# Turning activations into the next product's layout: ten of fourteen batches from TensorE transposes to VectorE block transposes and ScalarE moves

## The chip, the cores and the metric

The kernel runs on one core of one Trainium2 chip. Five engines work side by side, each from its own queue of instructions and in its order: TensorE (PE in the profile; its weight loads are PEld), VectorE (DVE), ScalarE (ACT), GpSimd (POOL), and SyncE (SP), which here does nothing but issue DMAs. The metric is the time of one execution on the device, in microseconds; the figure of a kernel is the median of several runs.

## The reference

One decoder layer over 256 tokens of 2048 channels, in float32. Three sub-layers follow each other, each on a normalised and modulated input, with a vector `mod` computed from a conditioning vector by a 2048 x 18432 product:

```python
mod = (silu(c) @ w_ada + b_ada).reshape(B, 9, 1, D)
h = modulate(rms_norm(x, g_ffn1), mod[:, 0], mod[:, 1])
x = x + 0.5 * mod[:, 2] * swiglu(h, w_ffn1_gu, w_ffn1_down)      # d_ff = 5632
h = modulate(rms_norm(x, g_mix), mod[:, 3], mod[:, 4])
u_pool, q, k, v, ga, gb = split(h @ w_in)
y_pool = multiscale_pool(u_pool, pool_mix, pool_scale) @ w_pool_up
y_attn = swa_sink_attention(q, k, v, ...) @ w_attn_up
merged = sigmoid(ga) * y_pool + sigmoid(gb) * y_attn
x = x + mod[:, 5] * (merged @ w_o)
h = modulate(rms_norm(x, g_ffn2), mod[:, 6], mod[:, 7])
x = x + 0.5 * mod[:, 8] * swiglu(h, w_ffn2_gu, w_ffn2_down)
```

with `swiglu(h) = (silu(h @ w_gate) * (h @ w_up)) @ w_down`.

## The kernel before

**Sets and ktiles.** Every large product is cut into sets. A set computes up to 1024 output columns for both token tiles (2 x 128 tokens) and walks the inner dimension in steps of 128 rows, called ktiles: 16 of them for inner dimension 2048, 44 for 5632. `Set.load` (L166) fetches 1 MB of weights by one DMA into a tile with the tag `raw`, of which there are six (`RAW = 6`): two ktiles of a 1024-wide set, four of a 512-wide one. `Set.prep` (L172) splits each ktile's float32 weights into a high half `wh`, cast on ScalarE (L180), and a low half `wl`, the difference taken on VectorE (L184); there are three buffers of each. `Set.mm` (L187) then runs, for each token tile, high x high (L194), low x high (L196) and high x low (L198): twelve matmuls for a 1024-wide ktile, six for a 512-wide one. The activations are the stationary operand and so must lie with their channels on the partitions. `run` (L205) walks a set and calls a hook after the ktile that the hook is registered for.

**Side work.** The `mod` vectors that are not needed at once are summed on VectorE while sets run: `ada_item` (L115) loads 1 MB of `w_ada` into another of the six `raw` tiles and adds it up by two instructions of 1024 columns (L129). `ada_side` sets how many such items follow each group of ktiles: 0.82 in the first FFN, 0.56 in the mixer, 0.15 in the second FFN.

**Turning.** A product's result has tokens on the partitions. In an FFN, for each block of 1024 columns (the last has 512), a gate set is followed by an up set; `silu_to` (L386, ScalarE) and `times` (L391, VectorE) leave the activated block in a tile `sg`, of which there is one. Before the down product it must be turned so that channels lie on the partitions, in the tile `actT` (tag `big`). `store_T` (L378) makes a list of pieces of two 128-channel blocks each; a piece, `pair_T` (L221), issues four 128x128 transposes on TensorE against an identity matrix (L225) into a PSUM bank and one copy on ScalarE (L382) from there to `actT`. `hook` (L397) registers the whole list behind ktile 3 of the next set. In the mixer the same is done by `tr` (L739) with the copy at L742: once per half of the merged block, during the gate-a set of the second half and during the first set of `w_o`.

There are fourteen such batches: three at once behind the first part of the first FFN, three more in that FFN (1024, 1024 and 512 columns), two in the mixer, six in the second FFN (five of 1024 columns, one of 512). The batch of columns 4096 to 5119 falls into the 512-wide gate set; the 512-column batch falls into the first set of the down product, whose activations are split by `split_stat` (L292; casts at L297, differences at L298).

**Order.** Each engine's order of instructions is fixed when the program is built, by a scheduler that weighs the order of the source against what it takes to be ready; so work can stand earlier in an engine's queue than its place in the source. Which buffer of a tag a tile gets is fixed then too, and the waits between engines follow from reads and writes.

Of the kernel before, what the change touches and what calls it, by code (L numbers as in the profile page):

```python
# [15 lines left out]
P = 128  # L16
D = 2048
# [22 lines left out]
def trunk_layer(ctx, tc, x, c, w_ada, b_ada, g_ffn1, w_ffn1_gu, w_ffn1_down, g_mix, w_in,  # L40
# [16 lines left out]

    # Eight PSUM banks in two groups of four: one holds the running set's accumulators, the
    # other serves everything small until the next set takes it.
    cur, rr = [0], [0]  # L60
# [7 lines left out]

# [1 line left out]
    ident = const.tile([P, P], F32, name="ident")  # L70
# [12 lines left out]

# [1 line left out]
    # Each partition sums its 16 rows of w_ada; a matrix of ones then sums the partitions.  # L85
    ada_v = w_ada[0].rearrange("(k p) n -> p k n", p=P)
# [12 lines left out]
    def mod_col(j, b, c0):  # L99
        """Sums that lie alike on all partitions, to a column for each 128 channels."""  # L100
        k, n = c0 // P, b.shape[1] // P
        d = t_([P, n, P], "t2", T2)
        nc.vector.tensor_tensor(d, b.rearrange("p (a q) -> p a q", a=n),
                                ident.unsqueeze(1).to_broadcast([P, n, P]), ALU.mult)
        m = mcol[:, j, k:k + n]
        nc.vector.tensor_reduce(m, d, AX.X, ALU.add)
        i, o = j // 3, j % 3
        bc = bcol[:, (2 * i + o) * KD + k:(2 * i + o) * KD + k + n]
        if o == 0:
            nc.vector.tensor_tensor(m, m, bc, ALU.add)  # L110
        else:
            nc.vector.scalar_tensor_tensor(out=m, in0=m, scalar=1.0, in1=bc, op0=ALU.add, op1=ALU.add)
            nc.vector.tensor_tensor(m, m, gcol[:, i * KD + k:i * KD + k + n], ALU.mult)

    def ada_item(j, c0, i, a):  # L115
        """An eighth of the sum for SW columns of one of the nine vectors."""
        if i == 0:
            a.append(t_([P, SW], "acc", 2))
            if j % 3 == 2:
                nc.gpsimd.memset(a[0], 0.0)  # L120
                nc.sync.dma_start(a[0][0:1, :], b_ada[0:1, j * D + c0:j * D + c0 + SW])
        raw = t_([P, 2, SW], "raw", RAW)
        nc.sync.dma_start(raw, ada_v[:, 2 * i:2 * i + 2, j * D + c0:j * D + c0 + SW])
        for k in range(2):
            sc = cs[:, 2 * i + k:2 * i + k + 1]
            if i == k == 0 and j % 3 != 2:
                nc.vector.tensor_scalar_mul(a[0], raw[:, k, :], sc)
            else:
                nc.vector.scalar_tensor_tensor(out=a[0], in0=raw[:, k, :], scalar=sc, in1=a[0],  # L129
                                               op0=ALU.mult, op1=ALU.add)  # L130
        if i < 7:
            return
        for o in range(0, SW, CW):
            b = bank()
            acc_sum(b, a[0][:, o:o + CW])
            if j % 3 == 2:
                if j not in gates:
                    gates[j] = t_([P, D], "gate", 1)
                nc.scalar.activation(gates[j][:, c0 + o:c0 + o + CW], b, AF.Copy, scale=1.0 if j == 5 else 0.5)
            else:  # L140
                mod_col(j, b, c0 + o)
# [12 lines left out]

# [1 line left out]
    class Set:  # L156
# [70 lines left out]

# [1 line left out]
    # sums of squares over D / 2, a last column holding twice EPS: their sum is twice the variance  # L229
    ssq = const.tile([P, T, 5], F32, name="ssq")  # L230
# [8 lines left out]
    def rsqrt2(v2, s0, r0, a):  # L239
        """r0 * a = 1 / sqrt(v2 / 2), by a Newton step from the engine's root."""  # L240
        nc.scalar.activation(s0, v2, AF.Sqrt, scale=0.5)
        nc.vector.reciprocal(r0, s0)
        if v2.shape[1] == 1:
            nc.vector.scalar_tensor_tensor(out=a, in0=v2, scalar=r0, in1=r0, op0=ALU.mult, op1=ALU.mult)
        else:
            nc.vector.tensor_tensor(a, r0, r0, ALU.mult)
            nc.vector.tensor_tensor(a, a, v2, ALU.mult)
        nc.vector.tensor_scalar(a, a, -0.25, 1.5, ALU.mult, ALU.add)
# [41 lines left out]

# [1 line left out]
    def split_stat(src, kept=None):  # L292
        """Halves of src, two ktiles at a time; some stay for another set if there is room."""
        cache = {}
# [32 lines left out]

    # ---- the last products of a phase and the first of the next, one token tile after the other,
    # so that each tile's sums, norm and transposes run under the other's products ----
    def tail(s, c0, jgate, after):  # L330
        """The last TAIL ktiles of a set; yields after each token tile's products."""
        items = []
# [45 lines left out]
    def store_T(src, f0, n, actT):  # L378
        """Transposes of act columns, to be called once the next set runs."""
        def dst(f, b):  # L380
            k = f0 // P + f
            nc.scalar.copy(actT[:, k:k + 2, :].rearrange("p a b -> p (a b)"), b)  # L382

        return [lambda f=f: pair_T(lambda t, f: src[:, t, f * P:(f + 1) * P], f, dst) for f in range(0, n // P, 2)]

    def silu_to(sg, g):  # L386
# [10 lines left out]
    def hook(fs):  # L397
        return {3: lambda: [f() for f in fs]} if fs else None

    def ffn(w_gu, w_down, hh, hl, actT, f0, pend, sg, g, jgate, after):  # L400
        """From act column f0 on, g holding the gate products there; up to the last set's tail."""
        stat = lambda k: (hh[:, k, :], hl[:, k, :])
        while f0 < DFF:
            fw = min(SW, DFF - f0)
            if sg is None:
                if g is None:
                    g = run(Set(w_gu, KD, (f0, fw), stat), hook(pend))
                    pend = []
                sg = t_([P, T, fw], "sg", 1)
                silu_to(sg, g)  # L410
                g = None
            times(sg, run(Set(w_gu, KD, (DFF + f0, fw), stat), hook(pend)))
            pend = store_T(sg, f0, fw, actT)
            sg = None
            f0 += fw
# [10 lines left out]

    # ---- first norm: its scale and shift come in column blocks, and with each block the
    # first sets of products go on; their sums wait in SBUF ----
    x_sb = const.tile([P, T, D], F32, name="x_sb")

    def ada_block(c0, w, shared):
        """The pieces of the first shift and scale at w columns. The rows of w_ada are summed on
        each partition, or, if shared, every other one goes through the tensor engine."""
        acc, banks = [], []
# [26 lines left out]
    nc.sync.dma_start(x_sb, x[0].rearrange("(t p) d -> p t d", p=P))  # L461
    # norm gains, pool scale and the biases of shifts and scales: a column for each 128 channels
    KG, KB = 3 * KD + PW // P, 6 * KD
# [68 lines left out]

# [1 line left out]
    WI = w_in[0]  # L534
    QO, KO, UO, GA, GB = PW, PW + NH * HD, 0, PW + NH * HD + 2 * NKV * HD, PW + NH * HD + 2 * NKV * HD + D

    # relative bias as a Toeplitz table in DRAM: column a holds distance a - 127
    rel = const.tile([NB + 1, NH], F32, name="rel")
# [63 lines left out]
    def qk_norm():  # L602
# [14 lines left out]
        for a in range(0, 8, 2):  # L617
            def dst(f0, b):
                nc.scalar.activation(qT[:, f0:f0 + 2, :].rearrange("p a b -> p (a b)"), b, AF.Copy, scale=gq[:, 0:1])
            pair_T(lambda t, f: q_sb[:, t, f * P:(f + 1) * P], a, dst)  # L620
        # keys and values in falling order of position
        b = bank()
# [47 lines left out]
    def heads_out(h0):  # L670
        l, kv = lg, h0 // 8
        pT = t_([P, 3, HB, P], "sg", 1)
        for i in range(HB):
# [3 lines left out]
            nc.scalar.copy(pT[:, :, i, :], b.rearrange("p (g q) -> p g q", g=3))  # L677
        # even heads fill the lower half of the partitions, odd heads the upper
        b1 = bank((P, 2, P))
# [43 lines left out]
    for half_ in range(2):  # L723
# [14 lines left out]

        def tr(sgb=sgb, half_=half_):  # L739
            def dst(f, b):  # L740
                k = half_ * 8 + f
                nc.scalar.copy(mT[:, k:k + 2, :].rearrange("p a b -> p (a b)"), b)  # L742
            for f in range(0, 8, 2):
                pair_T(lambda t, f: sgb[:, t, f * P:(f + 1) * P], f, dst)
        hk = {3: tr}
    residual(run(Set(w_o[0], KD, (0, SW), split_stat(mT)), hk), 0, 5, sumsq)
# [4 lines left out]

# [1 line left out]
    ov = out[0].rearrange("(t p) d -> p t d", p=P)  # L753
# [18 lines left out]
def _shape_constants():  # L772
    import numpy as np

    # pooling as a product over positions: mean over the window, less the token itself
    pw = np.zeros((4, P, TOE), np.float32)
    for g, w in enumerate(POOL_WINDOWS):
# [6 lines left out]
        pw[g, :, S:] = full[P:, P:]  # L784
    # bucket of each distance, one-hot; row NB marks what the window leaves out
    n = np.arange(TOE) - (P - 1)
# [33 lines left out]
```

## Time and profile before

| what | value |
|---|---|
| median of three runs | 2044.59 us (2043.46 to 2045.07) |
| span of the profiled execution | 2041.3 us |
| TensorE matmuls busy | 2008.7 us, 9053 instructions |
| VectorE busy | 1472.2 us, 1698 instructions |
| ScalarE busy | 987.3 us, 1324 instructions |
| read from HBM | 520.00 MB, 256 GB/s over the span |

The profiled execution's own time stands nowhere but in its span, from the first to the last instruction; the median of the runs is 3.3 us longer than that span, which is what lies around it. In the rows below, a row of a timeline gives the start in us, the duration, the engine, the line of the kernel, the operation, the tiles written and read, the shape and the count, and in brackets the idle time of the engine before it with what ended it. A row of the grouped lines gives, behind the bar, the busy time in us, the mean duration of one in ns, and the idle time before the group with what ended most of it. A row of waits gives who waited for whom, the us in total, how many times, and the longest.

### The profile page before, as it was taken

How to read it: one execution, taken by the hardware profiler on the slowest of the kernel's cores; microseconds unless marked ns; L12 is line 12 of the kernel's file. 1: busy time of each engine (PE TensorE's matmuls, PEld its weight loads, DVE VectorE, ACT ScalarE, POOL GpSimd, SP SyncE). 2: the span in 40 equal slices, each digit the busy share in tenths (PEclk: the TensorE clock that was granted, in tenths of full speed). 3: DMA queues.
4: the chain of work that ended last, by engine and by line, in shares of the span. 5: the costliest groups of instructions: out<-in, count | busy, mean ns of one | idle time of the engine just before them, and what ended most of it. 6: DMA issues, size and time to landing. Idle time of an engine off the chain costs nothing. (4 is left out here: it accounts for less than half of the span.)

```text
span 2041.3 us, 23823 instructions
## 1 busy us (share of the span) xinstructions
PE 2008.7 (98%) x9053; PEld 1648.5 (81%) x9053; DVE 1472.2 (72%) x1698; ACT 987.3 (48%) x1324; POOL 7.3 (0%) x17
## 2 busy tenths in 40 slices
PE   6999999999999999999999999999999999999999
PEld 4788888888788887888788887788888888888887
DVE  5799878788899956777878788755555555566645
ACT  3554454444544546546554455654443444454443
POOL 0000000000000000000000000000000000000000
PEclk9999999999999999999999999999999999999999
DMA  9988758998898855776868887455655656666762
GB/s 337 356 316 301 279 198 305 334 338 313 318 350 334 333 195 183 252 278 229 293 237 288 292 283 270 165 209 207 243 206 206 228 204 214 219 223 231 233 193 69
DMA packets 157915, 523.69 MB, mean 257 GB/s; under 512 B 9353, under 2 KB 23394, under 8 KB 157544
## 3 DMA queue, kind: packets, MB, share of 16 engines
q1 hardware_dynamic: 157800, 522.16, 72.2%
q8 instruction: 71, 1.16, 0.2%
q14 instruction: 44, 0.36, 0.0%
HBM read 520.00 MB, written 2.12 MB: 256 GB/s over the span
## 5 line engine op out<-in xcount | busy, mean ns | idle before, releaser
L180 ACT CAST wh<-raw 128x1024 fp32r<-128x1024 f32 (+2 forms) x731 | 730.9, 1003 | 949.6 <-PE bank L196 874.2
L184 DVE TENSOR_TENSOR wl<-raw,wh 128x1024 fp32r<-128x1024 f32 (+2 forms) x746 | 842.0, 1136 | 452.2 <-ACT wh L180 447.2
L194 PE MATMUL bank<-wh,hh 128*128 128x512 f32 x2072 | 654.5, 390 | 6.7 <-ACT hh L278 5.7
L198 PE MATMUL bank<-wl,hh 128*128 128x512 f32 x2072 | 651.8, 389 | 0.8 <-DVE wl L184 0.5
L196 PE MATMUL bank<-wh,hl 128*128 128x512 f32 x2072 | 652.1, 389 | 0.0
L194 PEld LDWEIGHTS bank<-wh,hh 128*128 128x128 f32 x2072 | 387.1, 188 | 88.4 <-ACT hh L278 7.8
L198 PEld LDWEIGHTS bank<-wl,hh 128*128 128x128 f32 x2072 | 389.0, 188 | 83.4 <-DVE wl L184 3.9
L196 PEld LDWEIGHTS bank<-wh,hl 128*128 128x128 f32 x2072 | 388.7, 188 | 81.5 <-DVE hl L279 1.4
L129 DVE SCALAR_TENSOR_TENSOR acc<-raw,cs,acc 128x1024 f32<-128x1024 f32 x216 | 276.4, 1279 | 41.2 <-DMA raw<-in_w_ada_dram 39.4
L198 PE MATMUL bank<-wl,sh 128*128 128x512 f32 x692 | 216.9, 390 | 1.9 <-DVE wl L184 1.9
L196 PE MATMUL bank<-wh,sl 128*128 128x512 f32 x692 | 216.6, 390 | 0.3 <-DVE sl L298 0.3
L194 PE MATMUL bank<-wh,sh 128*128 128x512 f32 x692 | 216.7, 390 | 0.0
L198 PEld LDWEIGHTS bank<-wl,sh 128*128 128x128 f32 x692 | 129.7, 188 | 29.6 <-DVE wl L184 2.8
L194 PEld LDWEIGHTS bank<-wh,sh 128*128 128x128 f32 x692 | 129.7, 188 | 28.6 <-ACT wh L180 0.6
L196 PEld LDWEIGHTS bank<-wh,sl 128*128 128x128 f32 x692 | 129.8, 188 | 27.9 <-DVE sl L298 1.0
L452 DVE SCALAR_TENSOR_TENSOR acc<-raw,cs,acc 128x1024 f32<-128x1024 f32 (+1 forms) x59 | 68.1, 1154 | 7.0 <-DMA raw<-in_w_ada_dram 6.2
L298 DVE TENSOR_TENSOR sl<-big,sh 128x512 fp32r<-128x512 f32 x88 | 60.0, 683 | 4.2 <-ACT sh L297 4.2
L297 ACT CAST sh<-big 128x512 fp32r<-128x512 f32 x88 | 54.3, 621 | 8.1 <-DVE big L652 8.1
L522 DVE TENSOR_TENSOR big<-bank,big 128x512 f32<-128x512 f32 x60 | 38.1, 682 | 1.2 <-PE bank L198 0.8
L276 ACT ACTIVATE t<-bank,mcol 128x128 f32<-128x128 f32 x90 | 35.0, 463 | 7.8 <-PE bank L264 7.1
L236 ACT ACTIVATE junk<-x_sb 128x512 bf16<-128x512 f32 x24 | 15.1, 629 | 19.9 <-DVE x_sb L322 13.8
L448 PE MATMUL bank<-raw,cs 128*128 128x256 f32 x64 | 19.4, 458 | 3.3 <-DMA raw<-in_w_ada_dram 3.3
(156 smaller groups left out, 698.2 us busy)
## 6 DMA issues: line engine op xcount, KB each, us to landing
raw<-in_w_ffn_gu_dram SPq DMA_DIRECT2D x176, 1024.0 KB, 5.0
raw<-in_w_ada_dram SPq DMA_DIRECT2D x112, 1024.0 KB, 6.4
raw<-in_w_ffn_down_dram SPq DMA_DIRECT2D x88, 1024.0 KB, 5.8
raw<-in_w_in_dram SPq DMA_DIRECT2D x48, 1024.0 KB, 5.0
raw<-in_w_ada_dram SPq DMA_DIRECT2D x64, 512.0 KB, 7.5
raw<-in_w_o_dram SPq DMA_DIRECT2D x16, 1024.0 KB, 7.1
raw<-in_w_pool_up_dram SPq DMA_DIRECT2D x8, 1024.0 KB, 6.9
raw<-in_w_attn_up_dram SPq DMA_DIRECT2D x8, 1024.0 KB, 5.6
```

Of the source, the lines that this page charges most:

```text
L129: nc.vector.scalar_tensor_tensor(out=a[0], in0=raw[:, k, :], scalar=sc, in1=a[0], op0=ALU.mult, op1=ALU.add)
L180: nc.scalar.copy(wh, raw_k)
L184: nc.vector.tensor_tensor(wl[:, e], raw_k[:, e], wh[:, e].bitcast(F32), ALU.subtract)
L194: nc.tensor.matmul(self.banks[t][i], hi[:, sl], wh[:, o], start=first, stop=False)
L196: nc.tensor.matmul(self.banks[t][i], lo[:, sl], wh[:, o], start=False, stop=False)
L198: nc.tensor.matmul(self.banks[t][i], hi[:, sl], wl[:, o], start=False, stop=last)
L276: nc.scalar.activation(h[:, f, :], src, AF.Identity, scale=g_, bias=b_)
L297: nc.scalar.copy(hi, src[:, k:k + n, :])
L298: nc.vector.tensor_tensor(lo, src[:, k:k + n, :], hi.bitcast(F32), ALU.subtract)
L448: nc.tensor.matmul(banks[j], sc.to_broadcast([P, P]), r[:, j, :], start=kk == 0, stop=False)
L452: nc.vector.scalar_tensor_tensor(out=acc[0], in0=r, scalar=sc, in1=acc[0], op0=ALU.mult, op1=ALU.add)
L522: nc.vector.tensor_tensor(a, b, a, ALU.add)
```

## The change

A new function `turn_T` takes the place of `store_T` in `ffn` (nine batches: three in the first FFN, six in the second) and of `tr` for the first half of the mixer. The three batches behind the first part of the first FFN and the second half of the mixer keep the TensorE transposes. In units of 1024 columns the ten batches are nine.

`turn_T` works in two steps. Behind ktiles 2 and 3 of the next set one VectorE transpose each, for one token tile, turns every 32x32 block of the activated block in place of the partition quarter where it lies, into a tile `z`, which is one of the six `raw` tiles. Behind ktiles 6 to 13 two ScalarE copies each move one of sixteen combinations (source quarter of 32 partitions, destination quarter) from `z` to `actT`: 32 partitions, and 512 elements on each of them for a 1024-column batch. Together they bring the blocks where a full transpose would have put them. No PSUM bank is used.

```diff
+    def turn_T(src, f0, n, actT):
+        z = []
+
+        def blocks(t):
+            if not z:
+                z.append(t_([P, T, n], "raw", RAW))
+            nc.vector.transpose(z[0][:, t, :], src[:, t, 0:n])
+
+        def move(i, j):
+            k, m = f0 // P, n // P
+            nc.scalar.copy(actT[32 * j:32 * j + 32, k:k + m, :].rearrange("p k (t i r) -> p k t i r", t=T, i=4)[:, :, :, i, :],
+                           z[0][32 * i:32 * i + 32].rearrange("p t (k j r) -> p k t j r", j=4, r=32)[:, :, :, j, :])
+
+        hk = {2 + t: (lambda t=t: blocks(t)) for t in range(T)}
+        moves = [lambda i=i, j=j: move(i, j) for i in range(4) for j in range(4)]
+        for k in range(6, 14):
+            hk[k] = lambda fs=moves[2 * (k - 6):2 * (k - 5)]: [f() for f in fs]
+        return hk
...
     def hook(fs):
-        return {3: lambda: [f() for f in fs]} if fs else None
+        return fs if not fs or isinstance(fs, dict) else {3: lambda: [f() for f in fs]}
...
             times(sg, run(Set(w_gu, KD, (DFF + f0, fw), stat), hook(pend)))
-            pend = store_T(sg, f0, fw, actT)
+            pend = turn_T(sg, f0, fw, actT)
...
-        def tr(sgb=sgb, half_=half_):
-            def dst(f, b):
-                k = half_ * 8 + f
-                nc.scalar.copy(mT[:, k:k + 2, :].rearrange("p a b -> p (a b)"), b)
-            for f in range(0, 8, 2):
-                pair_T(lambda t, f: sgb[:, t, f * P:(f + 1) * P], f, dst)
-        hk = {3: tr}
+        hk = (turn_T if half_ == 0 else lambda *a: hook(store_T(*a)))(sgb, half_ * SW, SW, mT)
```

## The prediction

> **What bounds the kernel now.** I read the page first, then the busy time by stages, then the chain of waits in one stage that the change touches, then what weight loads wait for.
>
> ```profile
> span 2041.3 us, 23823 instructions
> PE 2008.7 (98%) x9053; PEld 1648.5 (81%) x9053; DVE 1472.2 (72%) x1698; ACT 987.3 (48%) x1324; POOL 7.3 (0%) x17
> ```
> ```profile
> core 0: us, PE busy (x) PEld busy (x) DVE busy (x) ACT busy (x) POOL busy (x), PEclk, DMA share, GB/s
> 327.00:500.00 173.00, 173.00 (x789) 143.52 (x788) 139.69 (x132) 79.63 (x95) 0.00 (x0) 1.00 0.91 330
> 500.00:557.00 57.00, 56.72 (x254) 45.48 (x253) 48.47 (x65) 32.94 (x52) 0.00 (x0) 1.00 0.86 305
> 557.00:720.00 163.00, 163.00 (x722) 134.24 (x721) 149.59 (x159) 77.50 (x92) 1.91 (x2) 1.00 0.90 335
> 1081.00:1140.00 59.00, 58.35 (x266) 48.02 (x265) 46.61 (x48) 28.51 (x34) 0.00 (x0) 1.00 0.85 310
> 1350.00:1750.00 400.00, 400.00 (x1799) 332.01 (x1798) 214.92 (x189) 171.93 (x186) 0.00 (x0) 1.00 0.61 218
> 1750.00:1795.00 45.00, 45.00 (x209) 37.50 (x208) 25.41 (x37) 23.50 (x38) 0.00 (x0) 1.00 0.60 197
> 1795.00:1920.00 125.00, 125.00 (x557) 103.62 (x556) 80.37 (x82) 60.45 (x70) 0.00 (x0) 1.00 0.68 225
> ```
> ```profile
> by line: PE bank L198 32.4%; PE bank L194 32.2%; PE bank L196 32.2%; PE bank L225 3.5%
> ...
> 1403.74 0.46 PE bank L198 x2
> 1404.20 1.75 PE bank L225 x16
> 1405.94 0.47 PE bank L194 x2
> ```
>
> The first three windows are the first FFN from its turned batches on, the fourth the mixer set that turns its first half, the last three the second FFN. TensorE is busy throughout at the full granted clock. The chain of waits for 1400 to 1500 us consists of TensorE alone, and the transposes (L225) are 3.5% of it: two batches in 100 us. So TensorE time removed there is end time removed, as long as nothing else becomes late. The stages differ in their cover: in the second FFN VectorE is busy 54% (214.92 of 400) and ScalarE 43%; in the first, VectorE is busy 81 to 92% and the DMA engines 86 to 91%.
>
> **What goes.** One batch of 1024 columns and the one of 512, on TensorE:
>
> ```profile
> 1492.38 0.62 PE L198 MATMUL bank<-wl,hh 128*128 128x512 f32 x2
> 1492.84 1.91 PE L225 MATMUL bank<-ident,sg 128*128 128x128 f32 x16
> 1494.51 0.71 PE L194 MATMUL bank<-wh,hh 128*128 128x512 f32 x2
> ```
> ```profile
> 1805.65 1.03 PE L225 MATMUL bank<-ident,sg 128*128 128x128 f32 x8
> 1806.44 0.71 PE L194 MATMUL bank<-wh,hh 128*128 128x512 f32 x2
> ```
> ```profile
> L225 PE MATMUL bank<-ident,sg 128*128 128x128 f32 x176 | 21.3, 272 | 0.0
> L382 ACT COPY big<-bank 128x512 f32<-128x512 f32 x44 | 22.4, 609 | 0.1
> L655 DVE TENSOR_REDUCE am<-big 128x4 f32<-128x1024 f32 x4 | 4.8, 1206 | 0.0
> L127 DVE TENSOR_SCALAR acc<-raw,cs 128x1024 f32<-128x1024 f32 x8 | 6.0, 749 | 1.6 <-DMA raw<-in_w_ada_dram 1.6
> L129 DVE SCALAR_TENSOR_TENSOR acc<-raw,cs,acc 128x1024 f32<-128x1024 f32 x216 | 276.4, 1279 | 41.2 <-DMA raw<-in_w_ada_dram 39.4
> L662 ACT ACTIVATE big<-big,am 128x256 f32<-128x256 f32 x16 | 7.9, 495 | 0.0
> ```
>
> From the first transpose to the next weight matmul it is 1494.51 - 1492.84 = 1.67 us for sixteen, and 1806.44 - 1805.65 = 0.79 us for eight. Ten batches go, eight full ones and two of 512 columns: 8 x 1.67 + 2 x 0.79 = 14.9 us. That is the gross gain. One transpose lasts 272 ns in its row but costs 0.104 us, since they overlap. The Trainium skill (TensorE: Matmul & The Clock Gate, Part 4: PE-mode transpose) gives about 275 ns for one in a kernel's context; the row agrees with that as a duration, but taken as the cost it would make 144 x 0.275 = 39.6 us of gain, and an estimate of 2005 us. The gap between neighbours decides here.
>
> **What comes, on VectorE.** Two block transposes of 128x1024 a full batch, of which the trace has none. Nearest rows: the one-input TENSOR_SCALAR at 0.75 us, the one-input TENSOR_REDUCE at 1.21, the three-operand L129 at 1.28. I take 1.21, one input at one element a cycle; upper end 2.4 (each element handled twice), lower end 0.75. The row for it is VectorE's idle time in a ktile, below:
>
> ```profile
> 1485.51 1.22 DVE L184 TENSOR_TENSOR wl<-raw,wh 128x1024 fp32r<-128x1024 f32 x1 [0.69 <-ACT wh L180]
> 1488.23 1.23 DVE L184 TENSOR_TENSOR wl<-raw,wh 128x1024 fp32r<-128x1024 f32 x1 [1.50 <-ACT wh L180]
> ```
> ```profile
> 1481.70 1.05 ACT L180 CAST wh<-raw 128x1024 fp32r<-128x1024 f32 x1 [1.67 <-PE bank L196]
> ...
> 1493.53 2.04 ACT L382 COPY big<-bank 128x512 f32<-128x512 f32 x4
> ```
>
> A 1024-wide ktile takes 1488.23 - 1485.51 = 2.72 us. VectorE idles 1.5 us in it, ScalarE 1.67 us. With three `wh` buffers a cast starts when TensorE is done with L196 of the ktile three before its own; two ktiles and two matmuls (2 x 2.72 + 0.45) pass before it is needed, less the cast: about 4.8 us of cover, and for `wl` about 4.5. A 1.21 us transpose in each of two ktiles fits the idle time even before it uses the cover. In the second FFN this costs nothing; at 2.4 us each it would still be inside the cover.
>
> **What comes, on ScalarE.** Four copies from PSUM went (2.04 us, so 0.51 us each in a row, 0.61 alone); sixteen moves of 32 x 512 come. All ScalarE rows here go by elements per partition, so I take 0.51 us each, 8.2 us a batch; lower end 0.4, upper end 1.05 (the 1024-element cast), in case 128-byte runs stream at half rate. Two a ktile are 1.0 us in 1.67 us of idle time: hidden. At 1.05 they overrun by 0.43 us a ktile, 3.5 us over eight ktiles, still inside 4.8. The 512-column batches have moves of 256 elements (0.5 us by L662) and hide in the down set's ktiles.
>
> The moves need not wait for ktile 6: work that is ready early stands early in the queues, as the casts `hh` for later ktiles do at the start of the down set, seven within two ktiles:
>
> ```profile
> 1795.69 1.65 ACT L297 CAST hh<-big 128x512 fp32r<-128x512 f32 x3
> 1797.26 1.05 ACT L180 CAST wh<-raw 128x1024 fp32r<-128x1024 f32 x1
> 1798.21 2.18 ACT L297 CAST hh<-big 128x512 fp32r<-128x512 f32 x4
> ```
>
> **Added waits.** A move waits for the VectorE transpose; behind it on ScalarE stand the casts, and TensorE waits for those. The transposes stand behind side sums (L129) that themselves wait for DMAs. And the load that takes `z`'s tile waits on SP for the last move, with all later loads behind it.
>
> **Where cover is thin.** 512-wide sets have half the ktile, so half the idle time and half the cover:
>
> ```profile
> 510.27 0.62 ACT L180 CAST wh<-raw 128x512 fp32r<-128x512 f32 x1 [0.74 <-DVE wl L184]
> ```
> ```profile
> DVE wl L184 <- ACT wh L180: 4.7, 8, 0.7
> DVE acc L129 <- DMA raw<-in_w_ada_dram: 3.3, 3, 1.2
> ```
> ```profile
> PEld bank L198 <- DVE wl L184: 1.7, 4, 0.6
> ```
>
> These waits are of 500 to 557 us: TensorE already waits 1.7 us there for `wl`, so its cover is gone at times. With a cover of about 2 us, two transposes (2.4) and a side item (two L129, 2.6) in the same four ktiles overrun. I charge 1.2 us for that first-FFN batch; 0.3 for its twin in the second FFN, where sixteen moves and casts fill most of ScalarE; 0.3 for each of the other two first-FFN batches and 0.2 for the mixer's. Loss 2.3 us, and bounds for it are nothing and, if every gain outside the second FFN is lost with as much again in stalls, 2 x (1.67 + 1.67 + 0.79 + 1.67) = 11.6.
>
> **The raw tiles.** With `z` out, five are left. Page of the profile, DMA issues:
>
> ```profile
> raw<-in_w_ffn_gu_dram SPq DMA_DIRECT2D x176, 1024.0 KB, 5.0
> raw<-in_w_ada_dram SPq DMA_DIRECT2D x112, 1024.0 KB, 6.4
> ...
> raw<-in_w_ada_dram SPq DMA_DIRECT2D x64, 512.0 KB, 7.5
> ```
>
> In the first FFN 1.82 loads fall on 5.44 us (two ktiles), so a tile comes round every 6 x 5.44 / 1.82 = 17.9 us, with five every 14.9. Landing (6.4) and use over two ktiles (5.44) need 11.8. It holds, with 3.1 us to spare in place of 6.1. In the second FFN five tiles still give 27 us. So no charge.
>
> **Sum.** 14.9 - 2.3 = 12.6 us off the span, 2041.3 to 2028.7; with the 3.3 us that the median lies over the span, 2044.59 - 12.6 = 2032.0.
>
> **The rivals.** What weight loads waited for from 327 to 720 us:
>
> ```profile
> PEld bank L198 <- DVE wl L184: 2.1, 5, 0.6
> ```
>
> (1) *The thin stages give everything back, or more.* VectorE at 81 to 92% and DMAs near 90% in the first FFN speak for it, full cover in most of its sets (2.1 us of waits for `wl` in all from 327 to 720 us, 1.7 of them in the 512-wide sets) against it. Only the second FFN's 5 x 1.67 + 0.79 = 9.1 us stay: 2035.5; with as much again lost in stalls (5.8), 2041.3.
>
> The Trainium skill's rule for kernel authors speaks against the change on this ground (VectorE: DVE Perf Modes, Rules for kernel authors): a 128x128 transpose belongs on TensorE if PSUM will do as its destination, 32x32 ones on VectorE. Here the 32x32 path adds about 22 us to VectorE (18 x 1.21) and 73 us to ScalarE to save 14.9; no row of before shows whether any of it surfaces.
>
> (2) *Slower: `z` starves the weight stream.* If the moves stay at ktiles 6 to 13 and the load of ktile 14 gets `z`'s tile, the load starts about 1.5 us into ktile 11 (cast of 13 at the end of 10, then two moves), and needs its landing and a 1.05 us cast before ktile 14, 8.2 us after ktile 11's start. It is late by landing minus 5.6 us. At 5.0 nothing shows; at the 7.5 of the last row, 1.9 us in each of ten batches are 19 us, against 14.9: 2048.7, and slower beyond. It decides from a landing of 7.1 us on. Medians of 5.0 and 6.4 and early moves speak against it.
>
> (3) *No change*: (1) at its worst, and a third of the second FFN's gain (3.0) lost too: 2044.3. That the change does less than it says I hold for unlikely, as the transposes are on the chain itself.
>
> **Chances.** Forecast 0.62 (2028.5 to 2034.5), (1) 0.20 (to 2041.3), (3) 0.11, (2) 0.07. The range 2028 to 2041 keeps the forecast, the gross gain and nearly all of (1), about 0.8. About 0.2% (4 us) is what a measurement can tell from no change: faster 0.80, same 0.13, slower 0.07.
>
> **What would show it.** Right: L225 down by 144; no TensorE wait at the hooks in 1400 to 1750 us; block transposes near 1.2 us, moves near 0.5 apart. The charge in the 512-wide gate set shows as TensorE waiting for `wl`; (1) as such waits over the first FFN; (2) as ScalarE casts ended by weight DMAs. Wrong, if moves last over 1.05 us or TensorE idles in the second FFN's 1024-wide sets.

## The result, and the profile after

The kernel after takes 2068.04 us (median of four runs, 2064.77 to 2068.65) against 2044.21 us before (2043.46 to 2045.07): ratio 1.0117, interval 1.0103 to 1.0131. The forecast was 2032.0 with a range of 2028 to 2041. The time lies above the range and on the other side. In each run on record the time is about 1.8 us longer than the span (2068.53 and 2066.7 us in the profiled execution of after); so the 3.3 us between median and span in the table ahead are in part the difference between one execution and another.

The head of the page of after with its busy row, its groups for the new lines, then what weight loads and moves waited for (who, for whom, us in total, times, longest):

```profile
span 2066.7 us, 23679 instructions
PE 2004.9 (97%) x8909; PEld 1641.1 (79%) x8909; DVE 1492.6 (72%) x1718; ACT 1058.7 (51%) x1448; POOL 7.3 (0%) x17
```
```profile
L398 ACT COPY big<-raw 32x512 f32<-32x512 f32 x128 | 79.1, 618 | 27.2 <-DVE raw L394 25.4
L394 DVE STREAM_TRANSPOSE raw<-sg 128x1024 f32<-128x1024 f32 x16 | 19.8, 1236 | 0.0
L398 ACT COPY big<-raw 32x256 f32<-32x256 f32 x32 | 12.9, 403 | 4.1 <-DVE raw L394 3.7
L225 PE MATMUL bank<-ident,sg 128*128 128x128 f32 x32 | 4.0, 272 | 0.0
```
```profile
PEld bank L194 <- ACT wh L180: 29.5, 10, 7.1
ACT big L398 <- DVE raw L394: 29.1, 9, 5.2
PEld bank L198 <- DVE wl L184: 8.6, 14, 2.8
...
PEld bank L196 <- DVE sl L298: 5.4, 4, 2.8
```

The same view of before, of which the prediction showed stretches only:

```profile
PEld bank L198 <- DVE wl L184: 6.6, 13, 2.3
PEld bank L194 <- ACT wh L180: 2.5, 3, 0.9
```

The 144 transposes went (176 to 32), but the weight loads now wait in ten places for a cast (29.5 us), and the longest of these waits is 7.1 us. The second row is the reason to look for: ScalarE itself stood 29.1 us in front of moves whose block transposes weren't done.

Adding up, over all weight matmuls, by how much the start of one comes more than 227 ns after the start of the one before it (where that is a weight matmul too), gives 18.9 us in before and 59.2 in after: 40.3 more. Less the 14.9 us of transposes this is 25.4; the span grew by 2066.7 - 2041.3 = 25.4. So the gross gain was there, and all that is to be explained are 40 us of new waits.

Where they lie, by the start of a stage's first instruction in the traces (the stages are cut at the first `times` of a block and the first update of the residual; length of a stage in before, and the change of it in each kernel; the kernels beside after are told below):

| stage | before | after | pin | blocks | pin70 | best |
|---|---|---|---|---|---|---|
| first FFN, start to 498.5 (one batch) | 498.5 | +0.9 | -1.9 | -0.3 | -5.2 | -3.5 |
| its 512-wide gate set, to 522.3 (one batch) | 23.8 | +10.2 | +5.9 | +3.2 | +5.4 | +1.7 |
| its 512-wide up set, to 545.5 | 23.2 | -0.7 | -0.6 | -0.6 | -0.6 | -1.5 |
| first down set, to 669.4 (512-column batch) | 123.9 | +12.6 | +12.9 | +12.2 | +1.0 | +1.2 |
| rest of the first FFN, to 795.7 | 126.3 | +2.8 | +2.8 | +2.8 | +2.3 | +2.2 |
| mixer, to 1349.0 (one batch) | 553.3 | +3.5 | -1.7 | -1.8 | -4.5 | -4.2 |
| second FFN, to 1748.1 (four batches) | 399.1 | -5.9 | -7.1 | 0.0 | -7.1 | -7.1 |
| its 512-wide gate set, to 1794.3 (one batch) | 46.2 | +2.9 | +0.7 | +1.6 | +0.7 | 0.0 |
| its down sets, to the end (512-column batch) | 247.0 | -0.9 | -0.9 | 0.0 | -0.9 | -0.9 |
| span | 2041.3 | +25.4 | +10.1 | +17.1 | -8.9 | -12.1 |

The first row holds the start of the kernel, which differs by some 2 us between profiled executions whatever the kernel (the first mark, the first `silu_to` at 362.0 us in before, comes at -1.4 in pin70 and at +0.3 in best). In before70, a control without any turning that is told below, the first row is 3.2 us longer than in before; so this row is not read closely.

One loss close up, in the 512-wide gate set of the first FFN of after: ScalarE, and then TensorE (with a wait at the hook before it ahead).

```profile
507.79 6.27 ACT L398 COPY big<-raw 32x512 f32<-32x512 f32 x10 [3.41 <-DVE raw L394]
514.09 1.66 ACT L180 CAST wh<-raw 128x512 fp32r<-128x512 f32 x3
```
```profile
420.63 0.73 PE L194 MATMUL bank<-wh,hh 128*128 128x512 f32 x2 [2.05 <-ACT wh L180]
```
```profile
514.76 0.79 PE L194 MATMUL bank<-wh,hh 128*128 128x512 f32 x1 [6.20 <-ACT wh L180]
515.35 0.63 PE L196 MATMUL bank<-wh,hl 128*128 128x512 f32 x1
515.78 0.63 PE L198 MATMUL bank<-wl,hh 128*128 128x512 f32 x1
```

ScalarE stood idle for 3.41 us in front of a move that waited for its block transpose, then did ten moves in a row, and only then three casts; TensorE stood waiting for the first of them. The source asks for two moves behind each of eight ktiles; the scheduler put ten in one place, and nine and sixteen at the hooks before and after:

```profile
413.85 5.66 ACT L398 COPY big<-raw 32x512 f32<-32x512 f32 x9 [2.79 <-DVE raw L394]
```
```profile
567.00 6.61 ACT L398 COPY big<-raw 32x256 f32<-32x256 f32 x16 [3.68 <-DVE raw L394]
```

The ten come 0.627 us after one another. TensorE waited 6.20 us, and when it went on its matmuls came 0.43 us apart in place of 0.23: the granted clock (last number but two of these windows) was 0.50, and 0.61 behind the wait at 420.63 us.

```profile
420.70:424.10 3.40, 3.40 (x10) 2.68 (x11) 3.40 (x3) 3.33 (x6) 0.00 (x0) 0.61 0.03 7
514.70:520.00 5.30, 5.24 (x12) 4.08 (x13) 2.59 (x4) 5.18 (x10) 0.00 (x0) 0.50 0.01 3
```

Such a wait is paid twice: the twelve matmuls after it came 2.4 us late in all. Of the 59.2 us in after, 11.1 are such gaps of about twice the length (380 to 500 ns) and not waits; of the 18.9 in before, 2.1. The Trainium skill (TensorE: Matmul & The Clock Gate, Part 1: The HAM clock gate) says that the clock is halved after an idle window of about 3.4 us. The trace agrees for the wait of 6.20 us; but it shows a lower clock after one of 2.05 us too. And not every wait of that size lowers it: after one of 2.38 us, in the second FFN's 512-wide gate set, the granted clock stays at 1.00, as it does after one of 2.04 us at 503.72 us. How long a wait has to be can't be read from these.

```profile
1780.88 0.50 PE L194 MATMUL bank<-wh,hh 128*128 128x512 f32 x1 [2.38 <-ACT wh L180]
```
```profile
1781.00:1784.40 3.40, 3.40 (x15) 2.81 (x16) 2.96 (x5) 3.31 (x6) 0.00 (x0) 1.00 0.00 0
```

### The profile page after: what moved, and what is told of

It is laid out like the page before. It is cut to its first block, busy times and chain, and to the rows that moved or that the text cites. A ratio compares the mean times of both kernels' runs of the same rounds, so it can differ in the third digit from the quotient of the medians.

```text
span 2066.7 us, 23679 instructions
## 1 busy us (share of the span) xinstructions
PE 2004.9 (97%) x8909; PEld 1641.1 (79%) x8909; DVE 1492.6 (72%) x1718; ACT 1058.7 (51%) x1448; POOL 7.3 (0%) x17
## 5 line engine op out<-in xcount | busy, mean ns | idle before, releaser
L129 DVE SCALAR_TENSOR_TENSOR acc<-raw,cs,acc 128x1024 f32<-128x1024 f32 x216 | 276.4, 1280 | 21.6 <-DMA raw<-in_w_ada_dram 20.0
L398 ACT COPY big<-raw 32x512 f32<-32x512 f32 (+1 forms) x160 | 92.0, 575 | 31.3 <-DVE raw L394 29.1
L297 ACT CAST sh<-big 128x512 fp32r<-128x512 f32 x88 | 54.3, 622 | 37.4 <-PE bank L198 29.3
L298 DVE TENSOR_TENSOR sl<-big,sh 128x512 fp32r<-128x512 f32 x88 | 60.1, 685 | 5.2 <-ACT sh L297 4.8
L94 ACT CAST t<-acc 128x512 fp32r<-128x512 f32 x28 | 17.0, 619 | 21.7 <-DVE acc L129 18.4
```

The source lines that it names most:

```text
L297: nc.scalar.copy(hi, src[:, k:k + n, :])
L298: nc.vector.tensor_tensor(lo, src[:, k:k + n, :], hi.bitcast(F32), ALU.subtract)
L398: nc.scalar.copy(actT[32 * j:32 * j + 32, k:k + m, :].rearrange("p k (t i r) -> p k t i r", t=T, i=4)[:, :, :, i, :], z[0][32 * i:32 * i + ...
```

## The experiments

Two theories stood after the traces. **A**: the order of ScalarE's queue; moves in clumps put the casts behind the cover. **B**: the weight stream starves, since `z` holds one of six `raw` tiles. A third came in with the first FFN's down set, where after loses 12.6 us: **C**: VectorE has no room for the block transposes there.

The ratio of each run below is against before as it was timed again in the same round, with medians of 2040.0 to 2042.0 us; it is not the quotient with 2044.21. A span is that of the one profiled execution, and executions of one kernel differ by several us (before: 2036.7 to 2049.9 over these rounds); so a difference of a few us between two spans is not read by itself.

**pin: the moves where the source has them.** Each move is told to keep its place in the order of the program; nothing else changes.

```diff
-            nc.scalar.copy(actT[32 * j:32 * j + 32, ...
+            tc.keep_in_program_order(nc.scalar.copy(actT[32 * j:32 * j + 32, ...
```

> The changed kernel, each move kept in ScalarE's queue behind all that the source has before it (so two moves behind the casts of each of ktiles 6 to 13), nothing else. Theory A, ScalarE's order: moves that stand in clumps of up to sixteen ahead of casts make the 40 us of added TensorE waits; spread out they go, and with the 14.9 us of transposes gone the time is 2028 to 2036. Theory B, the weight stream starves with one raw tile out: z is held still longer here, so 2065 or more. Theory C, VectorE is late by the block transposes: they stay, so 2060 to 2070.

2050.65 us, ratio 1.0054 [1.0034, 1.0074], span 2051.4: 15.3 us of the 25.4 are gone (by the two ratios 0.63%, some 13 us). The time lies between the ranges of A and C, so neither is the whole. In the second FFN the moves now stand as the source has them, and the casts keep their beat of 2.72 us:

```profile
1424.96 1.25 ACT L398 COPY big<-raw 32x512 f32<-32x512 f32 x2
1426.60 1.05 ACT L180 CAST wh<-raw 128x1024 fp32r<-128x1024 f32 x1 [0.39 <-PE bank L196]
1427.68 1.25 ACT L398 COPY big<-raw 32x512 f32<-32x512 f32 x2
1429.32 1.05 ACT L180 CAST wh<-raw 128x1024 fp32r<-128x1024 f32 x1 [0.39 <-PE bank L196]
```

ScalarE keeps 0.39 us to spare in each ktile, where before it had 1.67; four batches give back 7.1 us there, 1.78 each. ScalarE's waits in front of moves for a block transpose fell from 29.1 to 3.3 us. A is shown for 13 to 15 us. The 12.9 us of the first down set stay.

**pool: the moves on GpSimd**, which is idle in before but for 7.3 us.

```diff
-            nc.scalar.copy(actT[32 * j:32 * j + 32, ...
+            nc.gpsimd.tensor_copy(actT[32 * j:32 * j + 32, ...
```

> The changed kernel with the sixteen moves of a batch on GpSimd in place of ScalarE; it is idle otherwise. Theory A: ScalarE's queue holds casts alone again, so the waits for wh go: 2028 to 2036, unless GpSimd takes over 2 us a move (z held over 32 us) or slows VectorE beside it. Theory B: z is held as long or longer, 2065 or more. Theory C: 2060 to 2070.

2078.91 us, ratio 1.0196 [1.0171, 1.0221], span 2075.0: slower than after. In the first batch the copies come 1.37 us apart (over the kernel they last 1.10 us on the mean), so that sixteen take 21.87 us, and the load that takes `z`'s tile waits on SP for the last of them. Timelines of GpSimd, SP and ScalarE:

```profile
412.74 21.87 POOL L398 COPY big<-raw 32x512 f32<-32x512 f32 x16 [185.35 <-DVE raw L394]
```
```profile
415.33 0.37 SPq L169 DMA_DIRECT2D raw<-in_w_ffn_gu_dram  x1
434.63 0.37 SPq L123 DMA_DIRECT2D raw<-in_w_ada_dram  x1
```
```profile
442.54 1.99 ACT L180 CAST wh<-raw 128x1024 fp32r<-128x1024 f32 x2 [9.42 <-DMA raw<-in_w_ffn_gu_dram]
```
```profile
ACT wh L180 <- DMA raw<-in_w_ffn_gu_dram: 45.4, 9, 9.4
```

SP issues nothing for 19 us, and a cast waits 9.42 us for its weights. Over the kernel there are nine such waits for gate and up weights, and seven more (21.1 us) for down weights; after has two for gate and up weights (18.9 us), as before has (19.9 us), at the start. This is B, the prediction's slower rival, as it described it; it happens when `z` is held for 22 us.

**raw5: five `raw` tiles in before**, without any turning.

```diff
-    RAW = 6
+    RAW = 5
```

> The kernel before with five raw tiles in place of six, all through. Theory A: the loads have slack, 2043 to 2049. Theory B: what z takes away for part of a set is taken away all the time, so at least as much is lost as the change lost beside its gain (40 us): 2075 or more. Theory C: 2043 to 2049.

2043.53 us, ratio 1.0013 [1.0003, 1.0024], span 2041.0. One tile fewer costs 0.13% by the medians and nothing by the spans, where B asked for 2075 us or more; B falls for after.

**blocks: the block transposes alone.** The kernel before, with the ten batches' block transposes on VectorE into a `raw` tile that nobody reads (behind ktile 3 for both token tiles); the TensorE transposes stay, and there are no moves.

```diff
+    def blocks_T(src, n):
...
+            nc.vector.transpose(z[0][:, t, :], src[:, t, 0:n])
...
+        return [lambda t=t: blocks(t) for t in range(T)]
...
-            pend = store_T(sg, f0, fw, actT)
+            pend = blocks_T(sg, fw) + store_T(sg, f0, fw, actT)
...
-        hk = {3: tr}
+        bl = blocks_T(sgb, SW) if half_ == 0 else []
+        hk = {3: lambda tr=tr, bl=bl: ([f() for f in bl], tr())}
```

> The kernel before with the block transposes of the ten batches added on VectorE into a raw tile whose content nobody reads; the TensorE transposes stay. Theory A: 2044 to 2048. Theory B: the raw tile is held only for the transposes, 2045 to 2055. Theory C: the same 40 us as the change lost, 2075 to 2085.

2061.49 us, ratio 1.0107 [1.008, 1.0133], span 2058.5, 17.1 above before. That is more than A allows and less than C's 2075. In the second FFN's 1024-wide sets they cost nothing, as predicted; in the first down set 12.2 us. So that loss comes with the block transposes, not with the moves. VectorE there in before and, behind its two transposes, in blocks:

```profile
558.66 1.22 DVE L184 TENSOR_TENSOR wl<-raw,wh 128x1024 fp32r<-128x1024 f32 x1
559.80 0.68 DVE L298 TENSOR_TENSOR hl<-big,hh 128x512 fp32r<-128x512 f32 x1
560.40 1.28 DVE L129 SCALAR_TENSOR_TENSOR acc<-raw,cs,acc 128x1024 f32<-128x1024 f32 x1
561.59 0.68 DVE L298 TENSOR_TENSOR hl<-big,hh 128x512 fp32r<-128x512 f32 x1
562.27 1.22 DVE L184 TENSOR_TENSOR wl<-raw,wh 128x1024 fp32r<-128x1024 f32 x1
```
```profile
557.51 1.29 DVE L392 STREAM_TRANSPOSE raw<-sg 128x512 f32<-128x512 f32 x2
558.73 4.26 DVE L298 TENSOR_TENSOR hl<-big,hh 128x512 fp32r<-128x512 f32 x7
562.91 1.28 DVE L129 SCALAR_TENSOR_TENSOR acc<-raw,cs,acc 128x1024 f32<-128x1024 f32 x1
...
567.11 2.35 DVE L184 TENSOR_TENSOR wl<-raw,wh 128x1024 fp32r<-128x1024 f32 x2
```

The transposes themselves take 1.29 us. But the order changed with them: where before puts one difference of the activations between two `wl`, blocks puts seven in a row, and no `wl` ends between 557.5 and 568. VectorE's busy time in the stage (third pair) of before, pin, and of pin70, which follows:

```profile
545.50:669.40 123.90, 123.90 (x549) 101.86 (x549) 117.21 (x129) 60.85 (x73) 0.96 (x1) 1.00 0.91 339
```
```profile
548.90:685.70 136.80, 129.70 (x543) 104.54 (x542) 122.00 (x135) 66.29 (x87) 0.95 (x1) 0.95 0.87 327
```
```profile
545.10:670.00 124.90, 122.97 (x540) 100.74 (x539) 112.37 (x121) 65.78 (x86) 0.00 (x0) 1.00 0.90 329
```

And what TensorE waited for in that stage of pin:

```profile
564.90 1.22 PE L194 MATMUL bank<-wh,hh 128*128 128x512 f32 x2 [3.39 <-ACT wh L180]
...
568.28 1.22 PE L198 MATMUL bank<-wl,hh 128*128 128x512 f32 x2 [1.30 <-DVE wl L184]
```
```profile
673.70 1.22 PE L196 MATMUL bank<-wh,sl 128*128 128x512 f32 x2 [2.39 <-DVE sl L298]
```

In before VectorE is busy 117.21 of 123.90 us. The change brings 1.4 us of transposes and, as work slipped in from the stages before (one side sum L129, one first sum L127 and one `wl` more), some more: 122.00. The wait of 3.39 us for a cast comes through ScalarE: the 3.3 us that it still stands in front of moves are these, eight moves follow, and the casts come behind them.

```profile
559.95 3.31 ACT L398 COPY big<-raw 32x256 f32<-32x256 f32 x8 [3.31 <-DVE raw L394]
...
563.81 2.94 ACT L180 CAST wh<-raw 128x1024 fp32r<-128x1024 f32 x3
```

So C has two readings, room (D1) and the order of VectorE's queue (D2).

**sel: fewer batches.** pin, with seven of the ten batches turned by `turn_T`: the first of the first FFN's three, the mixer's, and five of the second FFN (all but the one in the 512-wide gate set).

```diff
-            pend = turn_T(sg, f0, fw, actT)
+            pend = turn_T(sg, f0, fw, actT) if jgate == 8 and f0 != 4 * SW or f0 == 3 * SW else store_T(sg, f0, fw, actT)
```

> Pinned moves as in the run pin, but only for seven of the ten batches: the first turned batch of the first FFN, the mixer's, the second FFN's four that fall into 1024-wide sets and its last one. The two in the first FFN's 512-wide gate set and down set and the one in the second FFN's 512-wide gate set go back to TensorE. If what pin loses lies in those three places alone, the gains of the others by the stages of pin add up: 1.9 + 1.4 + 7.1 + 0.9 = 11.3 us off, ratio 0.993 to 0.996. If a loss moves to another place, 0.998 or more.

2037.53 us, ratio 0.9984 [0.9975, 0.9993], span 2035.9. A little faster than before, but 0.998 was the mark for a loss that moves elsewhere. The first down set still loses 4.8 us (from the differences of its two ends to before), though its batch is turned on TensorE: VectorE has more side sums there (33 again), is busy 120.08 of 128.70 us, and TensorE waits 2.39 us for `sl`, at 661.72 us. So a fuller VectorE costs time there without any block transpose.

**pin70: side sums later in the first FFN.** pin, with the rate at 0.70; **before70** is the kernel before with the same rate. What isn't summed in the earlier sets is summed behind the first down set, still in the first FFN: 37 side sums (L127, L129) there in place of pin's 17, while the mixer has 103 in both.

```diff
-    ada_side([(j, c) for j in (2, 4, 3) for c in (0, SW)] + [(7, 0)], 0.82)
+    ada_side([(j, c) for j in (2, 4, 3) for c in (0, SW)] + [(7, 0)], 0.70)
```

> pin with the side work of the first FFN at 0.70 items a group in place of 0.82, so that VectorE has 0.3 us a ktile less in the sets that turn. Theory D1, VectorE has no room there (117 of 124 us busy before): the 13 us that pin loses between the last up set and the end of the first down set fall to 3 or less, and the time is 2036 to 2043. Theory D2, it is the order in VectorE's queue (seven hl differences in a row ahead of wl): the loss stays, 2047 to 2054.

> The kernel before with the side work of the first FFN at 0.70, as the control of pin70. Both theories: no change, ratio 0.998 to 1.002; the side work then ends later in the down sets, where VectorE has room.

pin70 takes 2036.12 us, ratio 0.9975 [0.9966, 0.9984], span 2032.5; before70 2042.68 us, ratio 1.0011 [1.0002, 1.002], span 2042.0. That is where D1 puts pin70, and the control moves little, as expected. The rate alone is worth nothing, but under the change it takes out 18.9 us of span (14.5 between the medians); the first down set loses 1.0 us in place of 12.9, with VectorE busy 112.37 us there. Of the waits in that set, the one for a cast behind moves fell from 3.39 to 1.66 us, the one for `wl` from 1.30 to 0.27, and the one for `sl` went; none was for a DMA. The order behind the block transposes is the same in both kernels: five differences, a side sum, one difference, a side sum, two differences, and only then two `wl`. In pin70:

```profile
550.95 3.06 DVE L298 TENSOR_TENSOR hl<-big,hh 128x512 fp32r<-128x512 f32 x5
...
558.12 2.35 DVE L184 TENSOR_TENSOR wl<-raw,wh 128x1024 fp32r<-128x1024 f32 x2
```

So this order alone does not make the loss.

**pinhl: the order of the split instructions.** pin, with the casts (L297) and differences (L298) of the activations told to keep their place too, at the rate of 0.82.

```diff
-            nc.scalar.copy(hi, src[:, k:k + n, :])
-            nc.vector.tensor_tensor(lo, src[:, k:k + n, :], hi.bitcast(F32), ALU.subtract)
+            keep = tc.keep_in_program_order if kept is not None else lambda i: i
+            keep(nc.scalar.copy(hi, src[:, k:k + n, :]))
+            keep(nc.vector.tensor_tensor(lo, src[:, k:k + n, :], hi.bitcast(F32), ALU.subtract))
```

> pin with the casts and differences that split the activations in the down product (hh and hl, sh and sl) kept in the order of the source on ScalarE and VectorE, so that none stands ahead of earlier weights. Theory D2: the stall behind the run of hl differences goes, the loss in the first down set falls to 4 or less, 2038 to 2044. Theory D1: the work is the same and the loss stays, 2047 to 2054.

2045.32 us, ratio 1.0023 [1.0013, 1.0033], span 2043.8: between the ranges of D1 and D2. The first down set's loss falls from 12.9 to 8.3 us, and 7.6 us of span go in all. So where VectorE is full, the order of these instructions is worth about a third of that loss. The edit orders the casts on ScalarE as well as the differences on VectorE, so VectorE's share of that third isn't told apart. With pin70 this says that room decides, and that the order matters when room is short.

**after70: the rate without the pin**, the edit of pin70's rate on after.

> The kernel after, its moves left where the scheduler puts them, with the side work's rate in the first FFN at 0.70 in place of 0.82. If the two causes (order of the moves on ScalarE; room on VectorE in the first FFN) stand beside each other and add, the order still costs what pinning took out at 0.82 (15.3 us between the spans), so the span is near 2032.5 + 15 = 2048 and the stage t3 to the end of the first down set is within 2 us of before. If the lower rate alone were the remedy (the clumps only hurt because VectorE was late), the span is within 4 us of the pinned kernel at 0.70: 2032 to 2036. If the rate changes nothing without the pin, 2064 to 2068.

2057.18 us, ratio 1.0083 [1.0069, 1.0096], span 2055.4. None of the three cases: it lies 7 us above the additive one. The spans:

| | moves as scheduled | moves pinned |
|---|---|---|
| rate 0.82 | 2066.7 | 2051.4 |
| rate 0.70 | 2055.4 | 2032.5 |

Pinning is worth 15.3 us at 0.82 and 22.9 at 0.70; the rate 11.3 and 18.9. By the ratios it is 0.63% and 1.08%, 0.34% and 0.79%: the same picture. The two causes don't add: each cure works better when the other is in place.

**best: pin70 with the batch of the 512-wide gate sets turned on TensorE**, in both FFNs, so that eight of the ten batches move. **bestj** is the same with the sixteen moves in another order.

```diff
-            pend = turn_T(sg, f0, fw, actT)
+            pend = (store_T if f0 == 4 * SW else turn_T)(sg, f0, fw, actT)
...
-        moves = [lambda i=i, j=j: move(i, j) for i in range(4) for j in range(4)]
+        moves = [lambda i=i, j=j: move(i, j) for j in range(4) for i in range(4)]
```

> The pinned kernel at rate 0.70, with the batch that falls in the 512-wide gate set (of both FFNs) turned on TensorE as before: eight of the ten batches move (the first FFN's other two, the mixer's two, the second FFN's four). If the stage loss of 5.4 us in the first FFN's 512-wide gate set and the 0.7 us in the second's belong to that batch (block transposes and moves in a set with half the time per ktile), the span falls from 2032.5 to about 2026.5. If that loss belongs to VectorE being full whatever is turned, it moves to the next stage and the span stays at 2031 to 2034.

> As the one before it, with the sixteen moves of a batch in another order: two moves in a row now read different quarters and write the same destination quarter, where before they read the same quarter and wrote different ones. If the 0.62 us from one move to the next is paid for changing the destination quarter, pairs come down to about 1.05 us and the time stays the same or falls by up to 1 us; if it is the full duration of a 32-partition copy whatever its quarters, pairs stay at 1.25 us and the time is that of the one before within 0.2%.

best takes 2032.54 us, ratio 0.9964 [0.995, 0.9977], span 2029.3: faster than both kernels. (Its eight batches are two in the first FFN, one in the mixer and five in the second FFN; the expectation's list has the mixer's and the second FFN's wrong.) It gains 3.2 us of span on pin70 where some 6 were expected, and 4.9 from the first mark on, without the start: 3.7 in the 512-wide gate set, 0.9 in the up set behind it and 0.7 in the second FFN's gate set. The +1.7 that stays in the first of them isn't a wait: 121 matmuls start between its marks in place of 112, four of them of the side work (L96, L97), which in before fall into the stage ahead. bestj takes 2032.13 us, ratio 0.9959 [0.9945, 0.9973]: no difference. Its moves, and best's:

```profile
1406.41 1.25 ACT L398 COPY big<-raw 32x512 f32<-32x512 f32 x2
```
```profile
1406.20 1.25 ACT L398 COPY big<-raw 32x512 f32<-32x512 f32 x2
```

Two moves take 1.25 us whether they share the source quarter or the destination quarter.

**before90: more side sums in before**, at a rate of 0.90, as a test of room alone.

```diff
-    ada_side([(j, c) for j in (2, 4, 3) for c in (0, SW)] + [(7, 0)], 0.82)
+    ada_side([(j, c) for j in (2, 4, 3) for c in (0, SW)] + [(7, 0)], 0.90)
```

> The kernel before, with the side work's rate in the first FFN at 0.90 in place of 0.82: no block transposes and no moves, only more side sums on VectorE (and more side loads on SP) earlier in that FFN. VectorE's instructions in the stage t3 to the end of the first down set last 125.8 us in all before, in a stage of 123.9 us, and 130.6 us in the pinned kernel. If room on VectorE alone is what the change runs out of there, some four more side items of two instructions in the stages before and in this one make it late as well: 5 to 13 us longer, span 2046 to 2054. If the loss needs the block transposes' own place in the queue, the time stays within 3 us of before. The rate also adds 10% of side loads to DMA engines that are 91% busy, which would show as casts and side sums that wait for DMAs and not as matmuls that wait for the low halves.

2046.23 us, ratio 1.0019 [1.0007, 1.0031], span 2048.4 (the slowest of its ten executions was profiled). Between the two cases, some 4 us over before: the first down set is 1.6 us longer, the rest of the FFN 2.8 more. But the stage had 36 side sums in place of 32 and other reductions of the side work fewer, so that VectorE's instructions there sum to 125.6 us, as in before (125.8). So the experiment did not fill VectorE, and it says only that side sums as such don't cost the 12 us. The direction fits (TensorE waits 2.39 us for `sl` at 635.38 and 2.72 us for `wl` at 677.38 us, where before has no such wait), the size was not tested. The nearest to a test of it is sel: VectorE's instructions there sum to 129.2 us without a block transpose, and the set loses 4.8 us.

## Why the prediction was wrong, step by step

- **What goes: right.** 144 transposes went, and four batches of the second FFN gave 7.1 us with the moves pinned, against 4 x 1.67 = 6.7 predicted. The accounting of the waits closes with 14.9 us.
- **Block transposes: right in size** (1.236 us against 1.21), and right that they hide in the second FFN: blocks loses nothing there in 1024-wide sets.
- **Moves: size off.** 0.51 us each in a row was read off four copies of 128 partitions, as 2.04 / 4; but those overlap and start (2.04 - 0.61) / 3 = 0.48 us apart, while the moves don't overlap and come 0.627 us apart. Sixteen take 10.0 us and not 8.2. Alone this would have been hidden: 1.25 us in 1.67 of idle time.
- **The step that failed first: "The moves need not wait for ktile 6: work that is ready early stands early in the queues".** I counted this as an advantage, with the early `hh` casts as the example. Early in ScalarE's queue means ahead of the casts on which TensorE waits, and not two at a time but nine, ten or sixteen. Ten moves are 6.27 us, against a cover of 4.8 in a 1024-wide set and about 2 in a 512-wide one. The overrun of a pair in a ktile was worked out and that of a clump never was. The example was of another kind: seven early casts with a weight cast among them, behind which TensorE did not wait. Pinning is worth 15.3 us.
- **Added waits: named but not priced.** "A move waits for the VectorE transpose; behind it on ScalarE stand the casts" is what the row of 29.1 us shows. It needed the question how late the transpose could be on a VectorE that is 85% busy (48.47 of 57.00 us); the 3.41 us seen above are more than that set's whole cover of about 2.
- **Where cover is thin: right place, wrong by a factor.** 1.8 us were charged for the three batches of the first FFN. Even with the moves pinned, its 512-wide gate set loses 5.9 us and its first down set 12.9, beside the 1.67 and 0.79 that should have come back. I priced the transposes' own 2.4 us against idle time. In the down set they came with other work into a stage with 6.7 us left (123.90 - 117.21), and the order of what was there changed; at the rate of 0.70 the same set loses 1.0. After several of the stalls the clock was lower for the next matmuls too. So the loss term of 2.3 us was the second step that failed: with the moves pinned, the span still stands 22.7 us above the 2028.7 forecast, and lowering the rate takes out 18.9 of them.
- **The raw tiles: right.** raw5 has a span of 2041.0 against 2041.3, and SP's waits for moves in after (36.5 us in all, the longest 6.6) end no cast.
- **The rivals.** (1) was the right mechanism, waits for `wl` and `wh` in the thin stages of the first FFN; its upper end was set by "as much again lost in stalls", which no row supported. (2) didn't happen in after, where the casts that DMAs ended are the same two as before, but did in pool. No rival had ScalarE's order as the mechanism. Of the 38.0 us between the span forecast (2028.7) and after's, the order alone makes 15.3, room on VectorE alone 11.3, and the two together 7.6 more, by the table of spans; 3.8 stay.
- **Most of the gain can be had.** At the rate of 0.70 the eight batches of best are worth 2042.68 - 2032.54 = 10.1 us of median against before70; their transposes (6 x 1.67 + 2 x 0.79) are 11.6. The spans differ by 12.7 us, but the fastest execution of best was profiled and one of before70 that is slower than its median.

## What to carry to other kernels

When many small copies move to an engine that also feeds the bottleneck, ask where in that engine's queue they will stand, and price the longest run of them against the cover, not the mean per step against the idle time; if a scheduler orders the queue, fix their place. Before adding even 1 us to an engine that is nearly full in a stage (VectorE here: 94.6%, 117.21 of 123.90 us), make room there: side work that can be done later is moved first. A price is a bound only if a row says so.

## What was unexpected of the hardware

- Copies of 32 partitions on ScalarE come their full length apart: 0.627 us for 512 elements, while four copies of 128 partitions start 0.48 us apart at a similar length, and casts of 128x512 0.52 us apart ((2.18 - 0.62) / 3; both rows are quoted ahead of the result). Two explanations stay open, the 32 partitions and the scattered runs of 32 elements; the order of quarters is excluded by bestj.
- The block transpose of 128x1024 float32 takes 1.236 us, nearly a plain two-input operation's time; one of 128x512 takes 0.70.
- A TensorE wait of about 2 us can be enough to lower the granted clock (0.61 over the next 3.4 us after 2.05 us), but need not be (1.00 after 2.38 us); one of 6.2 us gives 0.50 over 5.3 us.
- A GpSimd copy of 32x512 lasts 1.37 us in a run of sixteen, and VectorE's `wl` beside it lasts 1.59 us each in place of 1.22 (one stretch of pool):

```profile
415.23 3.18 DVE L184 TENSOR_TENSOR wl<-raw,wh 128x1024 fp32r<-128x1024 f32 x2
```
